# Lp pooling in one dimension: a first piece twice as large, on other partitions, for 15 of the 16 DMA engines

## Chip, cores, metric

One core of one Trainium2 chip. The metric is the device time in microseconds (us). Medians are given with their range; all executions told here are of the state "fast" (granted clock 1.00).

## What is computed

```python
x: (32, 256, 4096) float32, p = 2, kernel_size = 4
window = np.abs(x[:, :, 4*i : 4*i+4]) ** p
result[:, :, i] = np.mean(window, axis=-1) ** (1 / p)      # (32, 256, 1024)
```

134.22 MB are read and 33.55 MB written. The kernel squares, adds in fours and takes the root of a quarter of the sum.

## The kernel before

The input is cut into blocks of 128 rows. Each load puts up to 13184 columns (52736 bytes a row) into one of three buffers; ScalarE squares, VectorE sums, ScalarE takes the root, and a store of two loads' results leaves.

```python
    W, O_W = 13184, 6592
    X_SLOTS, O_SLOTS = 3, 2
    slots = [[(W, [W])]] * 17 + [[(W, [6592, 6592])]]
    slots += [[(W, [5792, 7392])], [(10808, [6592, 2808, 1408])]]
    ODD = 840
    ...
    LAGS = {8: 2}          # (cut: one line with others) how long a group's root is put off
```

840 of the 262144 columns are not in these loads. They go first, as 30 rows of 14336 bytes, on 30 partitions (a partition is one of the 128 rows of the on-chip memory, SBUF). A DMA of 128 rows runs on all 16 engines here, one of 30 rows on 15 (16 and 15 completion packets in the trace), so this "first piece" gives 15 engines something that the 16th does not get.

```python
    Q = 30
    odd = ODD * P // Q
    t = o_tiles[1][0:Q, 0:odd]
    nc.sync.dma_start(out=t, in_=xf[(total - ODD) * P:total * P].rearrange("(p w) -> p w", p=Q))
    ahead = 0
    while ahead < n and loads[ahead][0] < X_SLOTS:
        load(ahead)                       # the first three big loads, on the same queue
        ahead += 1
    nc.vector.tensor_tensor(out=t, in0=t, in1=t, op=mybir.AluOpType.mult)
    o = o_tiles[1][0:Q, odd:odd + odd // k]
    nc.vector.tensor_reduce(out=o, in_=t.rearrange("p (n j) -> p n j", j=k), ...)
    nc.scalar.activation(out=o, in_=o, func=Act.Sqrt, scale=1.0 / k)
    stores["odd"] = nc.scalar.dma_start(out=..., in_=o)
```

## Time and profile before

| | |
|---|---|
| time, three executions before the prediction | 393.84 us (393.64 to 395.03) |
| profiled execution | 395.11 us, span 393.3 us |
| DMA | 167.77 MB, 427 GB/s over the span |
| VectorE, ScalarE | 70% busy each |

The time of an execution is 1.8 us more than its span (395.11 against 393.3). The prediction below shows the DMA lines, a table of stretches and the chain. Of the timeline (start, duration, engine, line, instruction, and in brackets how long the engine had been idle and what ended it) these lines answer to lines shown later:

```profile
4.96 3.88 DVE L137 TENSOR_TENSOR ot<-ot 30x3584 f32<-30x3584 f32 x1 [4.96 <-DMA ot<-in_x_dram]
...
20.60 11.19 ACT L167 ACTIVATE xt<-xt 128x13184 f32<-128x13184 f32 x1 [6.87 <-DMA xt<-in_x_dram]
```

The piece's arithmetic begins at 4.96 us and the first big square at 20.60. What no view prints are the single packets. The trace has a start, a duration, a size and a queue for each, but not the engine. A big packet is one row of 52736 bytes and takes 1.95 us when nothing disturbs it, 27.0 GB/s; each engine's last packet of a DMA is followed by a 4-byte completion.

### The profile page before, as it was taken

Reading aid. Unit: us, or ns where it says so; the run is one execution under the profiler, and the core shown is the slowest. Engines: PE = TensorE matmul, PEld = TensorE weight load, DVE = VectorE, ACT = ScalarE, POOL = GpSimd, SP = SyncE. Lnnn points to the kernel's source line nnn. Section 1 sums busy time; section 2 is a strip of 40 time slices with the busy share of each in tenths; the row PEclk is TensorE's granted clock in tenths of the full one; section 3 lists DMA queues with packets and bytes.
Section 4 is the critical chain, followed back from the end, with each engine's and each line's share of the span. In section 5 each row is a group of like instructions: output and inputs, shape, how many; then the busy total and the mean of one; then the engine's idle time right before and its main releaser. Section 6 shows DMA issues by size and latency. Waiting matters only on the chain.

```text
span 393.3 us, 182 instructions
## 1 busy us (share of the span) xinstructions
DVE 274.5 (70%) x36; ACT 275.4 (70%) x38; POOL 0.2 (0%) x4
## 2 busy tenths in 40 slices
DVE  4207898885869376948693869396929690989991
ACT  1095879919990899099809991998099809986991
POOL 0000000000000000000000000000000000000000
DMA  8999999999989999999999999999999899999996
GB/s 312 429 440 429 467 445 451 381 432 469 434 386 429 472 429 429 456 402 429 429 432 426 429 472 429 456 400 467 429 437 429 386 429 467 429 429 423 440 409 295
DMA packets 4554, 167.77 MB, mean 427 GB/s; under 512 B 526, under 2 KB 526, under 8 KB 556
## 3 DMA queue, kind: packets, MB, share of 16 engines
q1 hardware_dynamic: 3501, 144.04, 85.0%
q10 hardware_dynamic: 1053, 23.73, 14.0%
HBM read 134.22 MB, written 33.55 MB: 427 GB/s over the span
## 4 chain that ended last, share of the span: by engine, by line
DMA 54%; ACT 25%; DVE 19%; SPq 0%; issue 0%; ACTq 0%
DMA xt<-in_x_dram 54%; ACT xt L167 22%; DVE ot L111 14%; DVE xt L122 3%; ACT ot L102 3%; DVE ot L124 1%; DVE xt L124 1%; ACT xt L102 1%; SPq L82 0%; ACTq L99 0%; SPq L132 0%
## 5 line engine op out<-in xcount | busy, mean ns | idle before, releaser
L167 ACT ACTIVATE xt<-xt 128x13184 f32<-128x13184 f32 (+4 forms) x23 | 217.4, 9458 | 97.9 <-DMA xt<-in_x_dram 96.2
L111 DVE TENSOR_REDUCE ot<-xt 128x3296 f32<-128x13184 f32 x15 | 208.3, 13886 | 88.7 <-ACT xt L167 88.7
L102 ACT ACTIVATE ot<-ot 128x6592 f32<-128x6592 f32 x9 | 51.1, 5679 | 0.0
L122 DVE TENSOR_TENSOR xt<-xt 128x3296 f32<-128x3296 f32 (+5 forms) x9 | 34.5, 3834 | 16.9 <-ACT xt L167 16.8
L124 DVE TENSOR_TENSOR ot<-xt 128x3296 f32<-128x3296 f32 (+1 forms) x4 | 10.9, 2733 | 0.1
L143 ACT ACTIVATE ot<-ot 30x896 f32<-30x896 f32 x1 | 0.9, 948 | 10.8 <-DVE ot L139 10.8
L137 DVE TENSOR_TENSOR ot<-ot 30x3584 f32<-30x3584 f32 x1 | 3.9, 3880 | 5.0 <-DMA ot<-in_x_dram 5.0
L124 DVE TENSOR_TENSOR xt<-xt 128x1448 f32<-128x1448 f32 (+4 forms) x5 | 7.0, 1409 | 0.2
L102 ACT ACTIVATE xt<-xt 128x3296 f32<-128x3296 f32 (+3 forms) x4 | 5.8, 1445 | 1.1 <-DVE xt L124 1.1
L164 DVE TENSOR_TENSOR xt<-xt 128x5792 f32<-128x5792 f32 x1 | 6.2, 6184 | 0.0
L139 DVE TENSOR_REDUCE ot<-ot 30x896 f32<-30x3584 f32 x1 | 3.9, 3874 | 0.0
L143 ACT ACT_TABLE_LOAD x1 | 1.3, 1283 | 0.7 <-PEq L200 0.7
L200 POOL MEMSET const-bfloat16-1.0<- 128x1 bf16 x1 | 0.1, 101 | 0.0
L200 POOL MEMSET const-uint8-127<- 128x1 uint8 x1 | 0.1, 101 | 0.0
L200 POOL MEMSET const-float32-0.0<- 128x1 f32 x1 | 0.1, 98 | 0.2 <-issue 0.2
L200 POOL MEMSET const-float32-1.0<- 128x1 f32 x1 | 0.1, 98 | 0.0
## 6 DMA issues: line engine op xcount, KB each, us to landing
xt<-in_x_dram SPq DMA_DIRECT2D x19, 6592.0 KB, 31.6
out_dram<-ot ACTq DMA_DIRECT2D x7, 3296.0 KB, 27.4
out_dram<-ot SPq DMA_DIRECT2D x2, 3296.0 KB, 24.0
xt<-in_x_dram SPq DMA_DIRECT2D x1, 5404.0 KB, 24.1
out_dram<-xt SPq DMA_DIRECT2D x1, 1648.0 KB, 11.0
out_dram<-xt SPq DMA_DIRECT2D x1, 1351.0 KB, 6.6
ot<-in_x_dram SPq DMA_DIRECT2D x1, 420.0 KB, 4.2
out_dram<-ot ACTq DMA_DIRECT2D x1, 105.0 KB, 8.7
```

What stands on the lines that cost most here:

```text
L102: r = nc.scalar.activation(out=o, in_=o, func=Act.Sqrt, scale=1.0 / k)
L111: r = nc.vector.tensor_reduce(out=o, in_=v.rearrange("p (n j) -> p n j", j=k), axis=mybir.AxisListType.X, op=add,)
L122: r = nc.vector.tensor_tensor(out=h, in0=q[:, :, 0:2], in1=q[:, :, 2:4], op=add)
L124: r = nc.vector.tensor_tensor(out=o, in0=h[:, :, 0], in1=h[:, :, 1], op=add)
L137: nc.vector.tensor_tensor(out=t, in0=t, in1=t, op=mybir.AluOpType.mult)
L139: nc.vector.tensor_reduce(out=o, in_=t.rearrange("p (n j) -> p n j", j=k), axis=mybir.AxisListType.X, op=mybir.AluOpType.add,)
L143: nc.scalar.activation(out=o, in_=o, func=Act.Sqrt, scale=1.0 / k)
L164: r = nc.vector.tensor_tensor(out=v, in0=v, in1=v, op=mybir.AluOpType.mult)
L167: r = nc.scalar.activation(out=v, in_=v, func=Act.Square)
L200: nc = _bacc.Bacc("TRN2", target_bir_lowering=False, num_devices=1)
```

## The change

Its intent: the 16th engine is the last to finish in the profile, so the piece that the other 15 move instead is doubled. The 840 columns come out of the last load.

```diff
-    slots += [[(W, [5792, 7392])], [(10808, [6592, 2808, 1408])]]
-    ODD = 840
+    slots += [[(W, [5792, 7392])], [(9968, [6352, 2408, 1208])]]
+    ODD = 1680
@@
-    Q = 30
+    LOW, Q = 64, 60
     odd = ODD * P // Q
-    t = o_tiles[1][0:Q, 0:odd]
+    t = o_tiles[1][LOW:LOW + Q, 0:odd]
@@
-    o = o_tiles[1][0:Q, odd:odd + odd // k]
+    o = o_tiles[1][LOW:LOW + Q, odd:odd + odd // k]
```

The row stays 14336 bytes; there are four rows an engine instead of two, on partitions 64 to 123.

## The prediction

> **What bounds the kernel now.** I read the whole page first, then a table of stretches, then the chain of work that ended last, then the single packet records of the trace. The page's strip of 40 slices, with the DMA totals under it:
>
> ```profile
> DMA  8999999999989999999999999999999899999996
> GB/s 312 429 440 429 467 445 451 381 432 469 434 386 429 472 429 429 456 402 429 429 432 426 429 472 429 456 400 467 429 437 429 386 429 467 429 429 423 440 409 295
> DMA packets 4554, 167.77 MB, mean 427 GB/s; under 512 B 526, under 2 KB 526, under 8 KB 556
> ...
> xt<-in_x_dram SPq DMA_DIRECT2D x19, 6592.0 KB, 31.6
> ...
> ot<-in_x_dram SPq DMA_DIRECT2D x1, 420.0 KB, 4.2
> ```
>
> The DMA engines are full in every slice but the first and the last; VectorE and ScalarE are each 70% busy. The last line is the first piece, 420 KB, that the change doubles. The table of stretches (duration, then DVE and ACT busy with instructions in brackets, POOL, clock, DMA share, GB/s) says the same more sharply:
>
> ```profile
> 0.00:1.70 1.70, 0.00 (x0) 0.97 (x1) 0.20 (x4) 1.00 0.00 0
> 1.70:4.00 2.30, 0.00 (x0) 0.31 (x1) 0.00 (x0) 1.00 1.78 554
> 4.00:10.00 6.00, 5.00 (x2) 0.00 (x0) 0.00 (x0) 1.00 0.86 369
> ...
> 200.00:300.00 100.00, 69.19 (x6) 71.28 (x8) 0.00 (x0) 1.00 1.00 434
> ...
> 345.00:386.00 41.00, 37.74 (x16) 34.64 (x11) 0.00 (x0) 1.00 1.00 430
> 386.00:393.30 7.30, 0.00 (x0) 0.00 (x0) 0.00 (x0) 1.00 0.60 253
> ```
>
> A packet is booked whole in the stretch where it starts, so the 1.78 and 554 of the second row are not real; the mean of the two rows from 1.7 to 10 us is about 1.1 busy at 420 GB/s. What can be saved is at the two ends: nothing moves for 1.7 us, and the last 7.3 us run at 0.60. The chain of waits ends like this:
>
> ```profile
> 345.62 24.13 DMA xt<-in_x_dram
> 369.75 0.02 issue
> 369.77 5.71 ACT xt L167
> ...
> 385.40 0.50 ACT xt L102
> ```
>
> The last load lands at 369.75, sixteen microseconds of arithmetic follow, the last store is issued at 385.92. One would conclude that the end is set by arithmetic. The packet records contradict it: on 15 engines the last store's first packet starts 6 ns behind the preceding one (386.99 to 387.31 us), so they were never empty. **The end is the DMA engines' own backlog.**
>
> The same records show an unevenness that no view prints. Sorting the 4-byte completion packets of every DMA, 16 to a DMA, the median and second-last of the final store's are at 390.38 and 390.59 us and the last at 392.09. The last load shows the same: 367.63, 367.77, 369.34. One engine is 1.7 us behind the median and 1.5 us behind the next, and the span ends (393.3) 1.2 us after it. Followed back by its phase it seems to be the engine that takes no part in the first piece: it starts its first big packet at 2.86 us, the others theirs between 3.14 and 3.92, and the big packets are the same for all. It leads by 0.3 to 0.4 us until about 70 us, loses some 1.1 us there (packets of 2.22 and 2.77 us instead of 1.95) and another 1.2 us between 304 and 326 us (2.23, 2.27, 2.37, 2.18). I do not know what slows it.
>
> [...]
> [...] the first piece has 30 packets on 15 chains, and posts 15 completion packets, not 16.
> [...] Here one engine is slow[...]; the number of it is not in the records.
> [...] 14336 bytes took 0.54 to 1.06 us (first packets) and 0.77 to 1.09 (second ones, mean 0.92), against 0.53 at the rate of the big packets (52736 bytes in 1.95 us, 27.0 GB/s per engine).
>
> **The change, part by part.**
> *Bytes per engine.* One column of all 128 rows is 8 rows x 4 bytes on an engine when read, a quarter of that when written: 40 bytes. 840 columns fewer in the big loads and stores are 33,600 bytes less on each of the 16. The first piece gains 2 rows of 14,336 and 2 of 3,584, 35,840 bytes, on 15 of them. So the 16th engine loses 33,600 bytes, 33,600/27.0 = 1.24 us; the 15 gain 2,240 bytes, 0.08 us. Total bytes stay 167.77 MB.
> *The first piece's rate.* Two more packets per engine: at full rate 2 x 0.53 = 1.06 us[...]. The 15 engines get back 26,880 bytes of the last load, 1.00 us; the stores add two packets of 0.14 us and drop 6,720 bytes, 0.25 us, net 0.03. So the 15 end later by 0.1 us (full rate) or 1.0 us (half rate). Before, the packet that followed the piece took 2.3 to 2.7 us instead of 1.95 and ended about 6.03 us[...].
> [...]
> *VectorE and ScalarE.* The row count does not change the time of an instruction over partitions, so the multiply 3.88, the reduce 3.87 and the root 0.95 should stay; they start 1 to 2 us later (4.96 before), end near 15.5 instead of 13.7, and the first big square waits for its load until over 20 (20.60 before). Hidden. The small store of the piece takes four turns between big packets instead of two, 4 us longer to land; its buffer is written again after 60 us. Hidden.
> *The tail.* The last load's chunks shrink from 6592, 2808, 1408 to 6352, 2408, 1208. On the chain: 5.71 to 5.50, 3.60 to 3.47, 1.89 to 1.81, 1.58 to 1.53, 1.27 to about 1.1, 0.90 to 0.77, 0.54 to 0.47, 0.50 to 0.45: about 0.9 us less. It only raises the slack of the last store, as the engines are still working off their backlog.
> *Sum.* The end is the later of the 16th engine (392.09 - 1.24 = 390.85, plus 0 to 1.0) and the slowest of the 15 (390.60 plus 0.1 to 1.0).
>
> **The rivals.**
> A, half rate, and the collision costs its whole microsecond: 16th at 391.85, others at 391.6. Gain 0.25 us. [...]against: the 16th engine's first two packets were already slow (2.76 and 2.26 us)[...], so I may have the cause of such delays wrong.
> B, half rate and no collision: others end at 391.6, gain 0.5 us; the 15 are now the late ones and half the advantage is paid back at the start.
> C, full rate: the slow first packets are a start-up cost paid once, the new two run at 0.53. Others at 390.7, 16th at 390.85, gain 1.24 us. For it: the 16th engine paid 1.1 us too much in its first two packets, and the 15 also 1.1 us in their first three, as if all paid the same start-up.
> D, the late engine is one of the 15 after all: no catch-up, the change costs 0.1 to 1.0 us. Against it: the phase of a single packet chain that I could follow across the store's packets at 72, 86 to 98 us and again from 304 us.
> E, arithmetic sets the end: then the last load's landing counts, 369.34 against the later of 368.35 and 368.7, plus the 0.9 us of the shorter tail, gain 1.5 us. Against it: no gap before the last store's packets.
>
> **Range and chances.** Weights 0.25 A, 0.35 B, 0.3 C, 0.05 D, 0.05 E: -0.06 -0.18 -0.37 +0.03 -0.08 = -0.66 us, 0.17%. From the median 393.84: 393.2 us. The three times of before lie between 393.64 and 395.03, and the profiled execution took 395.11, so a median of a few runs may move by 0.5 us up for no reason of the change; the best rival puts it at 392.3. I take 392.4 to 394.3. To be over 2% faster would need 7.9 us; all that is not full-rate DMA at both ends is some 1.7 + 2.9 us, so 0.01. Slower by over 2% needs a stall that nothing here suggests: 0.01.
>
> **What would show it right or wrong.** The piece's issue-to-landing time should go from 4.2 to about 6.1 us under A and B, 5.3 under C. The first big square should start at 21 to 21.7 instead of 20.60, or 20.7 under C with the start-up paid once. The final store's last completion should be within 0.5 us of the next one, not 1.5. The stretch from 200 to 300 us must stay at about 434 GB/s. If the lag stays at 1.5 us, or the slow packets at 70 and 304 to 326 us move to another engine, my account of the late engine is wrong.

The sum came to -0.66 us, 393.2 us from the median, and the weights and gains stand as recorded; grounds of some terms are cut, since no trace shows them. Cut is how long the two added packets take at half rate, a term of the 1.0 us by which the 15 end later and so of the 391.6 and the landing at 6.1. Worked out from the second packets before (0.93 us on average, 1.09 at most) they would take 1.9 to 2.2 us, which less the 1.00 and plus the 0.03 is 0.9 to 1.2: an estimate that bears the 1.0 out. Cut as well is the ground of the collision in rival A and in "plus 0 to 1.0", the author's guess that the piece's rows on 64 to 123 hold up the 16th engine; its 1 us rests on nothing measured, and A's -0.06 is in the sum.

## The result

| | before | changed |
|---|---|---|
| median of six executions | 394.51 us | 395.29 us |
| range | 393.64 to 395.41 | 395.03 to 395.61 |
| profiled span | 393.3 us | 393.5 us |

The ratio is 1.002, 95% interval 1.0002 to 1.0038: about 0.8 us slower, which at a threshold of 2% is "the same", but outside the predicted range of 392.4 to 394.3. (Ratios are the mean time of one kernel's fast runs over that of the other's of the same rounds, so not quite the ratio of the medians quoted.)

The six times of before tell more than their median: 393.64, 393.84, 393.99, then 395.03, 395.05, 395.41. The changed kernel has no quick ones; all six lie where before's slow ones are.

From the page of the changed kernel, the DMA lines:

```profile
GB/s 264 429 451 429 429 429 429 426 472 389 434 450 477 434 429 429 389 469 429 394 464 429 434 426 429 432 429 461 397 472 450 399 437 466 429 429 410 412 429 341
...
ot<-in_x_dram SPq DMA_DIRECT2D x1, 840.0 KB, 6.5
```

The first slice moved 264 GB/s where it was 312, and the piece took 6.5 us from issue to landing instead of 4.2. The last slice is at 341 instead of 295: the end is less ragged. The table of stretches (columns as in the prediction) shows both ends:

```profile
1.70:10.00 8.30, 2.69 (x1) 0.31 (x1) 0.00 (x0) 1.00 1.02 313
200.00:300.00 100.00, 69.14 (x6) 68.82 (x8) 0.00 (x0) 1.00 0.99 430
...
386.00:393.50 7.50, 0.00 (x0) 0.21 (x1) 0.00 (x0) 1.00 0.73 309
```

The stretch from 1.7 to 10 us has a DMA share of 1.02 at 313 GB/s; in the kernel before it is

```profile
1.70:10.00 8.30, 5.00 (x2) 0.31 (x1) 0.00 (x0) 1.00 1.11 420
```

So the engines count as busy in both, but move a fifth less for the same share (313/1.02 against 420/1.11). **Busy is not moving.** And the timeline of the changed kernel, at its start and its end:

```profile
7.30 3.89 DVE L138 TENSOR_TENSOR ot<-ot 60x3584 f32<-60x3584 f32 x1 [7.30 <-DMA ot<-in_x_dram]
11.23 3.88 DVE L140 TENSOR_REDUCE ot<-ot 60x896 f32<-60x3584 f32 x1
15.14 0.95 ACT L144 ACTIVATE ot<-ot 60x896 f32<-60x896 f32 x1 [13.13 <-DVE ot L140]
...
23.05 11.19 ACT L168 ACTIVATE xt<-xt 128x13184 f32<-128x13184 f32 x1 [6.95 <-DMA xt<-in_x_dram]
...
370.10 5.48 ACT L168 ACTIVATE xt<-xt 128x6352 f32<-128x6352 f32 x1
...
376.43 3.46 DVE L122 TENSOR_TENSOR xt<-xt 128x3176 f32<-128x3176 f32 x1
...
385.76 0.45 ACT L102 ACTIVATE xt<-xt 128x302 f32<-128x302 f32 x1 [0.77 <-DVE xt L124]
```

Twice the rows cost the engines nothing (3.89, 3.88 and 0.95 us, as before), but the first big square begins at 23.05 instead of 20.60: 2.45 us were lost before anything else happened. The arithmetic after the last load takes from 370.10 to 386.21, as long as before (369.77 to 385.90) in spite of its smaller chunks, since VectorE, busy with the load before, reaches the new chunk at 376.43, 0.8 us after its square was done.

The packet records say where the 2.45 us went. For each kernel, the piece's packets are sorted by start and taken 15 at a time (the first 15 are each engine's first packet, and so on), with the mean duration of each fifteen; the completions give the end of the first load, the last load and the last store:

```
                                     before      changed
first, second packet, us          0.82, 0.93   1.10, 0.85
third, fourth packet, us                   -   1.10, 1.11   (all between 1.09 and 1.12)
the 15 start their big packets          3.61         6.04   (median)
first load's completions, median       19.93        22.34
last load's completions, median       367.63       369.19
final store's, median                 390.38       391.70
              second-last             390.59       391.88
              last                    392.09       392.21
```

14336 bytes at 27.0 GB/s would be 0.53 us. The two added packets run at half rate and cost 2.21 us (430,080 bytes, 195 GB/s for the 15 together); the first packet is 0.29 slower, the second 0.08 faster: 2.42. The last load is 1.00 us shorter per engine, so about 1.4 us stay for the 15, as the median completions show (+1.56 at the last load, +1.32 at the final store). The engine that was 1.5 us behind the next one is no longer last: what was gained there was spent on the other 15.

### The profile page after: what moved, and what is told of

Same layout as the page of the kernel before. It is cut to its first block, busy times and chain, and to the rows that moved or that the text cites. A ratio compares the mean times of both kernels' runs of the same rounds, so it can differ in the third digit from the quotient of the medians.

```text
span 393.5 us, 182 instructions
## 1 busy us (share of the span) xinstructions
DVE 273.7 (70%) x36; ACT 274.5 (70%) x38; POOL 0.2 (0%) x4
## 3 DMA queue, kind: packets, MB, share of 16 engines
q10 hardware_dynamic: 1083, 23.84, 14.1%
## 4 chain that ended last, share of the span: by engine, by line
DMA 44%; ACT 31%; DVE 21%; another core or an unknown queue 1%; issue 1%; ACTq 0%; SPq 0%
DMA xt<-in_x_dram 44%; ACT xt L168 26%; DVE ot L111 14%; ACT ot L102 4%; DVE xt L122 4%; DVE xt L165 2%; DVE xt L124 1%; ACT xt L102 1%; DVE ot L124 0%; ACTq L99 0%; SPq L133 0%; SPq L82 0%
## 5 line engine op out<-in xcount | busy, mean ns | idle before, releaser
L168 ACT ACTIVATE xt<-xt 128x13184 f32<-128x13184 f32 (+5 forms) x23 | 216.7, 9427 | 96.0 <-DMA xt<-in_x_dram 94.3
L122 DVE TENSOR_TENSOR xt<-xt 128x6592 f32<-128x6592 f32 (+6 forms) x9 | 34.1, 3784 | 15.5 <-ACT xt L168 15.4
L144 ACT ACTIVATE ot<-ot 60x896 f32<-60x896 f32 x1 | 0.9, 947 | 13.1 <-DVE ot L140 13.1
L138 DVE TENSOR_TENSOR ot<-ot 60x3584 f32<-60x3584 f32 x1 | 3.9, 3890 | 7.3 <-DMA ot<-in_x_dram 7.3
L140 DVE TENSOR_REDUCE ot<-ot 60x896 f32<-60x3584 f32 x1 | 3.9, 3882 | 0.0
```

What stands on the lines that cost most here:

```text
L122: r = nc.vector.tensor_tensor(out=h, in0=q[:, :, 0:2], in1=q[:, :, 2:4], op=add)
L168: r = nc.scalar.activation(out=v, in_=v, func=Act.Square)
```

## The experiments

Each kernel ran with one profile and, in timed rounds, beside the kernel before on the same chip. Theory P in the expectations is the guess that the rate of the piece depends on where its rows lie in the partitions. P-step and P-span are two forms of it: what counts is where the 15 engines write at the same moment, or how much of the partitions the piece covers in all.

### Noise, and a second profile: the kernel before, unchanged

> The kernel before, unchanged, against itself: the noise, and a second profile. Theory T (the time is set by whichever DMA engine is last; the 16th engine loses a varying time in some executions, and that makes the six earlier times of before fall into two groups, 393.6 to 394.0 and 395.0 to 395.4): the times fall into the same two groups, and if the profiled run is one of the quick ones the last engine of the final store is at most 0.5 us behind the next one, if one of the slow ones 1 us or more. Rival N (the two groups are chance): the lag of the last engine has nothing to do with the time.

Measured: 393.78 us (393.71 to 395.11), before on the same chip 394.33 (393.67 to 395.15), ratio 0.9993 [0.9976, 1.0010]. The profiled execution was a quick one: 393.71 us, span 391.9, and the final store's second-last and last completions are at 390.52 and 390.69 us. The slow one that I had read before predicting had 390.59 and 392.09. The other 15 engines are the same in both; only the last engine differs. So in these two profiles the difference in time goes with how much the last engine lost.

### The placement alone: 30 rows on partitions 64 to 93

```diff
-    Q = 30
+    LOW, Q = 64, 30
```

(with `LOW` added to the slices as in the change, 840 columns as before)

> The kernel before with its 30 rows on partitions 64 to 93: the placement alone, without the doubling. Theory P: [...]nothing changes: the piece lands at 4.2 us, and the times are spread as before's, 393.6 to 395.4 us. Rival C (the rows on the upper half get in the way of the 16th engine): its first big packet takes 3.4 us or more instead of 2.5 to 2.8, and the times move to the upper end, 395 us.

Measured: 394.34 us (393.62 to 395.77), ratio 0.9996 [0.9974, 1.0019]. The 16th engine's first big packet took 2.74 us (2.76 in the first profile of before), second packets of the piece 0.91 us on average. The placement does nothing, for better or worse. Its profile is of the slowest execution of the six and shows an engine 1.9 us behind.

### The doubling on the lower partitions: 60 rows on 0 to 59

```diff
-    LOW, Q = 64, 60
+    LOW, Q = 0, 60
```

> The changed kernel with its 60 rows on partitions 0 to 59. Theory P ([...]the piece at half rate, 1.10 us a packet, and the 15 start their big packets 2.4 us later than before): still 1.10 us a packet and 395.2 us, within 0.3 of the changed kernel, with only the 16th engine's first big packet back from 4.15 to about 2.8 us. Rival C (the collision of the piece with the 16th engine's rows is what costs the time): about 394.2 us.

Measured: 395.18 us (395.02 to 395.38), ratio 1.0021 [1.0007, 1.0036]; third and fourth packets 1.08 us. The same as the changed kernel: the loss comes with 60 rows, on either half. But one expectation failed: the 16th engine's first big packet, 4.15 us in the changed kernel, took 4.28 us here, although the piece now lies on the other half of the partitions. So a piece on the upper half, on which the prediction's rival A rested, is not what slows it. What does is not found.

### The same bytes on 105 partitions

```diff
-    LOW, Q = 64, 60
+    LOW, Q = 0, 105
```

> The changed kernel with the same 1680 columns on 105 partitions from 0, seven rows of 8 KB an engine[...]. Theory P: packets near 0.3 us, the piece lands in about 5.2 us instead of 6.5, the 15 start their big packets near 4.9 us instead of 6.0 and the kernel takes about 394.1 us, 1.1 less than the changed one. Rival S (the piece is slow since the DMA engines start cold or HBM reads are slow at first): landing at 6.3 or more, 395.2 us.

Seven rows of 8 KB an engine, 57344 bytes, as many as in the changed kernel (which addresses an engine reads is not in the records); what differs is where they land, and that a packet has 8192 bytes instead of 14336 (the run on partitions 32 to 91 below keeps the size). Measured: 393.88 us (393.73 to 394.00), before 394.33, ratio 0.9988 [0.9974, 1.0002]. The middle packets took 0.31 us (0.30 at 27.0 GB/s), later ones 0.41 to 0.44; the 15 start their big packets at 5.03 us. From its page:

```profile
ot<-in_x_dram SPq DMA_DIRECT2D x1, 840.0 KB, 5.5
```

1.3 us quicker than the changed kernel (by the two ratios to the kernel before), with the same bytes for each engine. Rival S, a slow start of the engines or of HBM, had the landing at 6.3 us or more and is out. All six executions are within 0.3 us.

### Still more partitions: 120

```diff
-    LOW, Q = 64, 60
+    LOW, Q = 0, 120
```

> The changed kernel with its 1680 columns on 120 partitions from 0, eight rows of 7 KB an engine. [...] Theory P-step[...]: the piece lands as late as with 60 rows, 6.3 to 6.5 us, and the kernel takes about 395.2 us. Rival P-span[...]: as with 105 rows, landing near 5.2 us, 393.9 us.

Measured: 394.91 us (394.83 to 395.13), ratio 1.0008 [0.9991, 1.0025]. 

```profile
ot<-in_x_dram SPq DMA_DIRECT2D x1, 840.0 KB, 6.4
```

The last two ranks of packets took 0.52 and 0.55 us for 7168 bytes (0.27 at full rate), the 15 start at 6.05 us. With 120 rows over both halves the piece is as slow as with 60 rows on one, so "more partitions" is not what helped the 105. P-span is out (6.4 us to the landing, 5.5 with 105 rows). That what counts is where the engines write at the same moment (P-step) remains the author's guess: no record has which engine writes which partition. That the partitions count, the next run tests.

### The decisive one: the same 60 rows on partitions 32 to 91

```diff
-    LOW, Q = 64, 60
+    LOW, Q = 32, 60
...
+    halves = [(32, 64), (64, LOW + Q)]
+    for lo, hi in halves:      # square on ScalarE, sum on VectorE; then both roots
```

Number and size of the rows are the changed kernel's; besides the partitions only the arithmetic differs: it is cut in two, as in the control below.

> The changed kernel with the same 60 rows of 14 KB, only on partitions 32 to 91[...]. The arithmetic of the piece is cut in two[...], and its squares go to ScalarE; it stays before the first big square. Theory P-step: packets of 0.53 to 0.6 us instead of 1.10, the piece lands near 5.2 us, 393.9 us. Rival M (60 rows of 14 KB are slow wherever they lie): 1.10 us a packet, 6.5 us, 395.2 us.

```profile
ot<-in_x_dram SPq DMA_DIRECT2D x1, 840.0 KB, 4.4
...
1.70:10.00 8.30, 1.63 (x1) 5.13 (x3) 0.00 (x0) 1.00 1.02 409
```

The first line is from its page, the second from its table of stretches: the same DMA share of 1.02 as in the changed kernel, at 409 instead of 313 GB/s.

Third and fourth packets took 0.54 us, all of them between 0.535 and 0.545. The piece of 840 KB landed almost as fast as 420 KB did before (4.4 us against 4.2). **The half rate of the changed kernel comes from the partitions that its rows lie on (1.10 us a packet on 64 to 123, 0.54 on 32 to 91), and, with the control, from nothing else that was changed here.** The time did not follow as expected, though: 394.78 us, in two groups of three, 394.3 and 395.2 to 395.5; ratio 1.0014 [0.9996, 1.0033]. Its control ran beside it on the same chip.

### Control: the cut arithmetic with the rows on 0 to 59

> The control for the run on partitions 32 to 91: the same cut arithmetic, but the rows on partitions 0 to 59. Theory P-step: 1.08 to 1.10 us a packet and 395.2 us, as with the rows on 0 to 59 and uncut arithmetic. If the cut arithmetic matters by itself, it differs from 395.2 by more than 0.3.

Measured: 395.42 us (395.35 to 395.71), ratio 1.0027 [1.0013, 1.0042]; packets 1.11 and 1.12 us, and in the same two views

```profile
ot<-in_x_dram SPq DMA_DIRECT2D x1, 840.0 KB, 6.4
...
1.70:10.00 8.30, 0.00 (x0) 3.12 (x2) 0.00 (x0) 1.00 1.00 313
```

Cutting the arithmetic changes nothing in the piece.

The time is 2.0 us more than the span here and with the rows on 32 to 91, 0.2 more than for kernels with uncut arithmetic, so spans are compared: 393.3 to 393.7 us in the control, 392.3 in the three quick executions on 32 to 91. That is 1.0 us less. But the median of the first big packets' ends was 1.77 us earlier (6.61 against 8.38), and the final store's median completion only 0.96 (390.69 against 391.65). Some 0.8 us were given back on the way.

### Where the rest went: putting off the first big store

In the packet records of the run on 32 to 91, 29 big packets that start between 71.5 and 75.3 us took 2.1 to 2.6 us instead of 1.95. Their excess over 1.948 us adds up to 9.2 us, 0.6 us for each of 16 engines. The control has none. The first big store was issued shortly before, from the timeline of the run on 32 to 91:

```profile
69.84 0.37 ACTq L99 DMA_DIRECT2D out_dram<-ot  x1
```

```diff
-    FINE, ENDS, LAGS = {19}, {18}, {8: 2}
+    FINE, ENDS, LAGS = {19}, {18}, {0: 2, 8: 2}
```

> The kernel with 60 rows on partitions 32 to 91, with the root and the store of the first group put off by one big square, so that the first big store is issued about 11 us later (near 82 instead of 71 us). Theory W (the packets of 2.1 to 2.6 us in all engines between 71 and 75 us are brought on by the start of the first big store): they move to about 83 to 87 us or go away. Rival L (they belong to that load or to that time): they stay at 71 to 75 us. Summed excess there before: 9.2 us over 16 engines, 0.6 us each; if they go away the time falls from 394.3 in quick executions to about 393.7.

```profile
85.44 0.37 ACTq L99 DMA_DIRECT2D out_dram<-ot  x1
```

The slow packets moved with the store: none from 66 to 80 us, 17 of them from 87.1 us on, 1.6 us after the issue, excess 6.9 us. So the store's issue, or the root put off with it, brings them on (Theory W), not the load or the moment in the kernel. It is not the store's own packets that are in the way: the first of these starts at 89.42 us, and 16 of the 17 slow load packets start before it. The time did not fall: 394.73 us (394.29 to 396.49), ratio 1.0023 [1.0000, 1.0045]; the profiled execution, a slow one, has two more such clusters at 130 and 150 us. By the span, the three quickest executions are at 391.9 to 392.2 us, 0.1 to 0.4 less than the 392.3 above; the time is 2.4 us more than the span in this run, for a reason not found.

The same with 840 columns on partitions 32 to 91, first without and then with the later store:

> 840 columns on partitions 32 to 91, 60 rows of 7 KB. Theory T with P-step: 0.27 us a packet, and the 15 engines are quick, but the 16th has nothing to make up its loss with: the times are spread, 394.0 to 395.4 us, as with 840 columns on 105 rows (394.2 to 395.4). Rival: if 840 columns at full rate are enough, 393.4 us and no spread.

Measured: 395.23 us (394.99 to 395.61), ratio 1.0022 [1.0007, 1.0037]. Packets of 7168 bytes took 0.28 us, landing 3.0 us after the issue: the quickest piece of all, and one of the slowest kernels. The excess between 66 and 78 us is 16.6 us, 1.0 for each engine, and the last engine ends at 392.41 us, 1.7 behind the median.

> The same putting off, on the kernel with 840 columns on partitions 32 to 91, where the excess was largest (16.6 us over 16 engines between 66 and 78 us, 1.0 us each). Theory W: moved to about 81 to 85 us or gone; Rival L: still at 69.8 to 75 us. If gone, the 15 engines' last store ends near 389.8 instead of 390.75 us, but the 16th still sets a time of 394.3 us or more.

Measured in four executions: 395.59 us (393.80 to 396.17), ratio 1.0024 [0.9995, 1.0052]. The slow packets moved to 85.4 to 89.8 us (store issued at 84.04), with the same excess of 16.5 us, and this profile too has another cluster, at 148 to 152 us. Moved, not removed. My hope that the time would come back was wrong in both.

Sorting the profiles by how early the first load was in (median completion) shows a pattern, not a smooth one, without explaining it. Packets over 2.05 us count as slow:

| kernel | first load in, us | excess of slow big packets, 66 to 78 us |
|---|---|---|
| no piece | 18.20 | 14.1 |
| 840 columns on 32 to 91 | 19.25 | 16.6 |
| 840 columns on 105 rows | 19.47 | 8.6 |
| 30 rows on 64 to 93 | 19.72 | 4.3 |
| before, two profiles | 19.77, 19.93 | 4.9, 2.3 |
| 1260 columns on 105 rows | 20.28 | 8.4 |
| 1680 columns on 32 to 91 | 20.45 | 9.2 |
| 1680 columns on 105 rows, two profiles | 21.12, 21.15 | 0.5, 0.2 |
| control, rows on 0 to 59 | 22.00 | 0 |
| 120 rows | 22.27 | 0 |
| changed | 22.34 | 0 |
| 60 rows on 0 to 59 | 22.63 | 0 |

### Is there a late engine at all: no piece

The piece, its arithmetic and its store are taken out; the last load has 11648 columns.

> No first piece at all: the 840 columns go back into the last load. Theory T (the 16th engine loses 1 to 2.5 us in every execution, and the piece of 15 engines is what makes up for it): the 16th engine is 1.0 to 2.5 us behind the others at the end in the profile, and every execution is slower than the quick ones of before: 394.6 to 396.0 us. Rival N (no engine is slow as such): all engines end within 0.6 us of each other, and the kernel takes 393.7 us or less, as nothing is lost at half rate.

Measured: 395.56 us (394.94 to 396.04), ratio 1.0021 [1.0001, 1.0042]. No quick executions are left, so the piece of before does earn its place. In the profile the last engine is 1.2 us behind the median but only 0.5 us behind the second-last, less clear than expected; and the 15 themselves are late, with the largest excess but one of the table and a wait for the last store's issue (0.5 us between its packets and the preceding ones). Rival N, 393.7 us or less, is out; that one engine alone makes the difference is not shown by this run.

### Sizes between, on 105 rows

840 columns:

> The kernel before with its 840 columns on 105 partitions from 0, rows of 4 KB. Theory P: the piece takes about 0.5 to 0.8 us less, landing near 3.6 instead of 4.2 us, and the quick executions are some 0.5 us shorter than before's, near 393.2; the slow ones, set by the 16th engine, are the same as before's. Rival S: within 0.2 us of before.

Measured 394.92 us (394.21 to 395.38), ratio 1.0014 [0.9997, 1.0031]: no quicker than before, and the piece landed at 4.0 us, not at 3.6. The last engine is 1.15 us behind the next (391.91 and 390.76). 1260 columns:

> 1260 columns on 105 partitions, rows of 6 KB: halfway between the two sizes that ran on 105 rows. Theory T with P: the 15 engines end between those of the two runs, near 390.7 us, and the 16th, with 16.8 KB less than with 840 columns, 0.6 us earlier than there: most times between 393.7 and 394.4 us. If the size is a flat optimum: within 0.2 us of the 1680 columns on 105 rows, 393.9.

Measured 394.20 us (393.98 to 395.09), ratio 0.9993 [0.9975, 1.0012]; the last two completions at 391.10 and 391.20. So in these profiles a larger piece nearly at full rate does bring the last engine in; the doubling was right in its aim. And 1680 columns on 105 rows again, on another chip:

> The quickest kernel so far, 1680 columns on 105 partitions, once more on another chip: 393.7 to 394.0 us with a spread of at most 0.4, against the kernel before's 393.7 to 395.5.

Measured 393.87 us: five of six between 393.83 and 393.98, one at 395.76; before 393.91 (393.71 to 395.29), ratio 0.9995 [0.9976, 1.0015]. It is the best version of those I ran, but it does not beat the kernel before clear of noise: it avoids most slow executions (11 of its 12 in two runs took 394.0 us or less, against 11 of 22 of the kernel before beside them) and is as quick as the quick ones.

## Why the prediction was wrong

- **"From the median 393.84: 393.2 us": the wrong base.** The gains were worked out against the profile, an execution of 395.11 us with an engine 1.5 us behind. Two of the three executions behind the median were quick ones, in which that engine is about 0.2 us behind (390.69 against 390.52 in the quick profile). I subtracted from 393.84 a lag that was not in it. On its own terms rival B ends at 391.6, plus 1.2 us to the end of the span and 1.8 us to the time: 394.6, not 393.3. This step alone puts the result outside the range. In a quick execution there was next to nothing to gain, and what the 15 lost (1.3 us at the final store) showed in full: hence slower, where quicker was forecast.
- **"Half rate" for the two added packets: right as a rate, too small as a cost.** Half rate was measured (1.10 and 1.11 us against 0.53), 2.21 us for the two (195 GB/s), and the piece's first packet was 0.29 us slower too. Why it is half was not shown before the change, and is not after it. The 15 start 2.42 us later; after the 1.00 us of the last load it is 1.3 to 1.5 us, where I had 1.0. Rival C, full rate, is out for these rows, and is what partitions 32 to 91 give (0.54 us).
- **"The collision costs its whole microsecond" (rival A): refuted as a cause.** The 16th engine's first packet was slow (4.15 us) but just as slow (4.28) with the piece on the other half.
- **"The 16th engine 390.85":** the changed profile has one engine ahead of the next by 1.0 us at the first load (21.22 against 22.21) and by 0.7 us at the end (390.92 against 391.63). If it is the 16th, as its phase suggests (the engine that starts with a big packet is the first to complete every load, by 0.99 us at the first and 0.6 or more at all later ones), the number was right, though not its parts: the longer piece held it up, too (first packet done at 7.58 instead of 5.62 us), and in this execution it lost little later.
- **"VectorE and ScalarE hidden": right**, to the duration. **"0.9 us less in the tail": not realised** (16.1 us both times), but without consequence: the final store's packets follow the preceding ones without a gap, as before. So rival E was rightly set aside.
- **The announced signs:** "last completion within 0.5 us of the next": 0.33 us, right. "First big square at 21 to 21.7": 23.05, wrong, and the plainest warning. "Landing about 6.1": 6.5. "200 to 300 us at about 434 GB/s": 430, and 433 in the quick profile of before's kernel. The slow packets of 70 and 304 to 326 us did not come back in the changed kernel (one of 2.29 us at 152.8); those at 70 came with the issue of the first store, the rest is open.
- **The chances** (0.98 for within 2%) were right; the range was not.

Open: what makes one engine lose 0.2 to 2 us in some executions; why loads slow down after the issue of the first big store in kernels that are early (excess of 2.3 to 16.6 us) and not in those that are late (0 to 0.5 us); what stretches the 16th engine's first packet; and why half of the executions with rows on 32 to 91 are 1 us slower. Nor do I have the number of the late engine: that it is the one without a share in the piece rests on its phase. A count agrees: if each packet of the first profile of before is chained to the one that starts as it ends, the engine that starts with a big packet gets 279 packets, as many as one without a share must have (the others have 6 more), and ends last, at 392.1 us; 16 of its steps are near ties.

## What to carry to other kernels

When a profile and a median come from different executions, first ask which of them the profile is: two groups of times that lie as far apart as the lag in the profile suggest that the gain from removing the lag belongs to one group only. A DMA that is given to fewer engines to balance them is worth trying on more than one set of partitions (here the same 60 rows took 1.10 us a packet on 64 to 123, 1.08 on 0 to 59, 0.54 on 32 to 91); compare the duration of its packets with bytes over the full rate (here 1.10 against 0.53 us), as the busy share looks the same in both (1.02 here, at 313 and at 409 GB/s). And balance is worth no more than the slowest of the others: here 1.3 us was paid on 15 engines to gain, at best, 1.5 on one.

## What else the runs show

- Covering more partitions was not enough for the full rate: 120 rows over both halves ran at half rate (0.52 to 0.55 us for 7168 bytes), 105 rows nearly at full rate (0.31 us for 8192 in the middle), 60 rows at full rate on 32 to 91 (0.54 us for 14336) and at half rate on 0 to 59 or 64 to 123 (1.08 to 1.11). Where the rate was half, it was so for all 15 engines: no third or fourth packet was faster than 1.09 us on 64 to 123, 1.065 us on 0 to 59. The cause is not shown.
- Loads slowed down for some microseconds after the issue of a store, before the store's first packet starts: in the four runs with the piece on 32 to 91, 17 to 33 packets of 2.1 to 2.8 instead of 1.95 us, from 1.3 to 1.7 us after the issue of the first big store, and moved with it from 71.5 to 87.1 us. The changed kernel has none.
- An engine's first big packet was slower beside a piece that it had no part in: 3.9 to 4.3 us with a slow piece, 3.3 to 3.6 with a quick one of the same bytes, 2.4 to 2.8 with half the bytes. The last is no more than the first packets take without a piece (2.1 to 2.9).
